# The last MLP's first matrix as seven block products of half-sized pieces, with sums of weights made by adding transfers

## The chip, the cores and the metric

The kernel runs on one core of a Trainium2 chip. The metric is the device time of one execution in microseconds (us). Before the change it is 2378.59 us, the median of 3 runs (2377.44 to 2379.38). The core's engines are TensorE (PE: matmuls; PEld is its weight load), VectorE (DVE), ScalarE (ACT), GpSimd (POOL) and SyncE (SP, which issues the DMAs here). Each runs its own queue in order.

## What is computed

A trunk of two layers over 1024 tokens of width 1024, in float32. Layer 0 mixes tokens with an mLSTM, layer 1 with latent attention over a shared K/V. Each mixer and each MLP stands between a norm with a modulation (scale and shift from a condition) and a norm with a gate. What the change touches is the MLP of the last layer (shortened):

```python
def sqrelu_mlp(h, w1, w2):                 # w1: 1024 x 4096, w2: 4096 x 1024
    return jnp.square(jax.nn.relu(h @ w1)) @ w2

for l in range(DEPTH):                     # two layers
    ...                                    # mixer
    h = modulate(rmsnorm(x, norm_g[l, 2]), sh2, sc2)
    y = sqrelu_mlp(h, mlp_w1[l], mlp_w2[l])
    x = x + g2[:, None, :] * rmsnorm(y, norm_g[l, 3])
return x
```

## The kernel before

**Precision.** Every large product is made of three fp32r matmuls: an operand is split into a rounded part `hi` and the rest `lo`, and `mm3` (L230) adds lo·hi, hi·lo and hi·hi into one PSUM tile (L231, L232, L233). Stationary tiles are 128x128, the moving operand is up to 512 columns wide.

**Weights.** `wload` brings 512 KB of weights (128x1024) into one of 4 `raw` buffers by a DMA on SP's queue; `wsplit` makes `wh` by a cast on ACT (L189) and `wl` by a subtraction on DVE (L190), in 8 buffers of the tag `ws`. The loads are issued AHEAD = 2 steps before their use.

**Stages.** Tokens are handled in two halves of 512 (`hfs[0]`, `hfs[1]`). Four MLP passes follow one another: `mlp(0, hfs[0])`, `mlp(0, hfs[1])`, `mlp(1, hfs[0])`, `mlp(1, hfs[1])`. `two_streams` runs the first three as a dense stream, between whose steps it puts the steps of mixers, of attention and of small preparations; the first has the preparation of latent weights beside it (`bg_latent`, which stores split weights to DRAM: the DMAs `lw<-wh` and `lw<-wl`). The last pass runs alone, with `all_out` (turning the residual stream into rows, `x_to_rows`, and the final norm, `rows_out`) between its steps.

**An MLP pass.** `mlp` makes a list of steps. A `hidden` step computes one of 32 blocks of 128 hidden features for 512 tokens: 8 blocks of input features, each `mm3` of 512 columns, so 24 matmuls into a PSUM tile `ps`; then relu (L962) and square (L963) on ACT, a cast (L471) on ACT and a subtraction (L472) on DVE give the two parts in `hd`. An `up` step multiplies hidden blocks with W2, 24 matmuls of 512 columns into `pm`, and adds the result to `y` (L198 on DVE). In the last pass the steps go in groups of four hidden blocks, and the `up` steps of a group stand between the hidden steps of the next one. A scheduler then orders each engine's instructions; `prompt` and `tc.high_priority` move weight loads and evacuations ahead, and `paced` holds others behind a given instruction. PSUM has two tiles each of `ps` and `pc` (one bank) and of `pm` (two banks).

Of the kernel before, what the change touches and what calls it, by code (L numbers as in the profile page):

```python
# [82 lines left out]
def kernel(  # L83
# [143 lines left out]

    pe_last = [None]

    def mm3(o, lh, ll, rh, rl, start, stop):  # L230
        nc.tensor.matmul(o, ll, rh, start=start, stop=False)  # L231
        nc.tensor.matmul(o, lh, rl, start=False, stop=False)  # L232
        pe_last[0] = nc.tensor.matmul(o, lh, rh, start=False, stop=stop)  # L233


    nc.scalar.preload_act_table_set("natural_log_exp_and_others")
# [240 lines left out]
    def normed(h, xs_, rstd, A, sh):  # L477

        for k in range(KD):
            with paced():  # L480
                nc.vector.scalar_tensor_tensor(
                    xs_[k], xs_[k], A[:, k : k + 1], rstd, ALU.mult, ALU.mult
                )
                split_mod(h.hi[k], h.lo[k], xs_[k], sh[:, k : k + 1])
            if k % 4 == 3:
                yield 1

# [455 lines left out]
    NF = DFF // P  # L943
    AHEAD = 2

    def mlp(l, hf, y, sizes, rows=False):


        w1, w2, h = mlp_w1[l], mlp_w2[l], hf.h2
        hids = {}  # L950

        def hidden(f):
            def hid(w):
                t = hdv(F32R)
                pt = ps()
                for k in range(KD):
                    if k == KD // 2:
                        yield "within"
                    mm3(pt, w[0][:, k], w[1][:, k], h.hi[k], h.lo[k], k == 0, k == KD - 1)
                s = tmp()  # L960
                with tc.high_priority(PRIO):
                    nc.scalar.activation(s, pt, AF.Relu)  # L962
                    nc.scalar.activation(s, s, AF.Square)  # L963
# [88 lines left out]
        steps, prev, f0 = [], [], 0  # L1052
        for G in sizes:
            fs = list(range(f0, f0 + G))
            f0, done = f0 + G, 0
            for i in range(G):
# [7 lines left out]
        for n in range(len(steps) + AHEAD):  # L1064
            if n < len(steps):
                ready.append(steps[n][0]())
            if n >= AHEAD:
                yield from steps[n - AHEAD][1](ready.pop(0))

                yield steps[(n - AHEAD + 1) % len(steps)][1].__name__  # L1070


    rope_d = scratch([2, P, S], "rope_d")
# [494 lines left out]

    def x_to_rows(half):

        for k in range(KD):
            a, b = tmc(), tmc()
            nc.sync.dma_start(a, xs_blk(k, half))
            yield
            pt = pc()
            for t in range(4):
                nc.tensor.transpose(pt[:, ts(t, P)], a[:, ts(t, P)], ident)
            nc.scalar.copy(b, pt)
# [19 lines left out]
    def rows_out(hf, y, B):  # L1598

        xt = []  # L1600
        for t in range(4):
            a = k4v()
            r0 = hf.i * H + t * P
            nc.sync.dma_start(a, xr[r0 : r0 + P, :].rearrange("p (a b) -> p a b", b=512))
            xt.append(a)
        yield
        for t in range(4):
            yt, st = y.t[t], small(4)
            for g in range(2):
                junk = ps()  # L1610
# [9 lines left out]
            for g in range(2):  # L1620
                nc.vector.scalar_tensor_tensor(ys[g], ys[g], r, xt[t][:, g], ALU.mult, ALU.add)
                r0 = hf.i * H + t * P
                nc.sync.dma_start(out[0, r0 : r0 + P, ts(g, 512)], ys[g])
            yield


# [126 lines left out]
    A1 = gain(2, NG(0, 2), adac(0, SC2))  # L1753
    B1 = gate(3, NG(0, 3), adac(0, G2))

    def post(hf, y, B, src, A, sh):
# [5 lines left out]
        yield 0  # L1762
        hf.h2 = Split()
        yield from normed(hf.h2, y, rstd, A, sh)

# [112 lines left out]
    def behind(fill, per):  # L1878

        more = True  # L1880
        while more:
            yield "align"
            more = some(fill, per)
            yield 1

    f0 = mlp(0, hfs[0], z0, [4] * 8)
    for n in range(20):
        if next(f0) != "within":
            next(p1, None)
    drain(p1)  # L1890
    two_streams(f0, behind(bg_latent(), 4))
    rope_perm()


    z1 = FH(claim=True)
    ya = [None, None]

    def mixer1(hf, z, attention):
# [12 lines left out]
        for _ in wout(b_w_out[0], hf.o, lambda m, pt: evac(y[m], pt)):  # L1911
            yield 0
        yield 1
        yield from post(hf, y, B2, x_cols, A3, adac(1, SH2))

    two_streams(mlp(0, hfs[1], z1, [2] * 14 + [4]), mixer1(hfs[0], z0, attention_first), bg_rest())


    u0 = FH(claim=True)
    two_streams(mlp(1, hfs[0], u0, [2] * 16, True), mixer1(hfs[1], z1, attention_second))  # L1920
    u1 = FH(claim=True)

    def all_out():
        yield from x_to_rows(0)
# [6 lines left out]

    fill = all_out()
    v = None
    dense = mlp(1, hfs[1], u1, [4] * 8, True)
    while (d := go(dense)) is not end:
        if v != "last" and d != "within":
            v = next(fill)
    drain(fill)

# [28 lines left out]
```

## Time and profile before

| what | us |
|---|---|
| median of 3 runs | 2378.59 |
| the profiled execution | 2377.5 |
| its span, first to last instruction | 2375.5 |
| POOL, L1346 memsets (32, attention's) | 6.6 |
| last pass, L472 on DVE (32) | 22.1 |
| last pass, L190 on DVE (61) | 74.6 |

The granted TensorE clock is 0.997 on average over the span. The profiled execution lies 1.1 us under the median of the runs. In a timeline a row gives start, duration, engine, line, operation and the tiles, output before input; what stands in square brackets is the time for which the engine had been idle and what ended that. Rows of matmuls overlap, since a matmul's duration runs to its end in the array; what one costs in a stream is read from start to start.

### The profile page before, as it was taken

To read this page: it belongs to the slowest core of one execution; us is meant where nothing else is said; L and a number is where in the kernel's file an instruction comes from. 1 tells how busy PE (TensorE), PEld (TensorE's weight loads), DVE (VectorE), ACT (ScalarE), POOL (GpSimd) and SP (SyncE) were. 2 spreads that over 40 slices of the span, in tenths; PEclk is the share of its full clock that TensorE was granted. 3 is DMA by queue.
4 is the path that set the end of the run, shared out by engine and by line. 5 is a ranking of instruction groups with operands and counts; after the bars stand their busy time and mean duration, and the time that the engine had idled before them with its cause. 6 is when DMAs were issued, how large, how long until landed. Compare 5 with 4: busy or idle time off the path is not lost.

```text
span 2375.5 us, 30534 instructions
## 1 busy us (share of the span) xinstructions
PE 2343.4 (99%) x11621; PEld 1946.7 (82%) x11621; DVE 1549.6 (65%) x2435; ACT 1055.6 (44%) x1716; POOL 18.2 (1%) x93
## 2 busy tenths in 40 slices
PE   7999999999999999999999999999999999999998
PEld 5888888788888888888888888888888888888887
DVE  6667866868666667877764967765666486353345
ACT  4355334655333454434443554444444453444333
POOL 1000000000000000000000000000000000000000
PEclk9999999999999999999999999999999999999999
DMA  9452664544664745555543454874434354364431
GB/s 313 149 142 85 186 181 139 168 133 144 186 181 143 250 135 187 160 161 183 182 133 113 147 166 163 249 248 136 148 98 143 114 169 129 102 191 140 144 102 62
DMA packets 377106, 374.48 MB, mean 158 GB/s; under 512 B 24355, under 2 KB 282464, under 8 KB 376960
## 3 DMA queue, kind: packets, MB, share of 16 engines
q1 hardware_dynamic: 376672, 372.44, 50.3%
q8 instruction: 91, 1.49, 0.3%
q14 instruction: 55, 0.45, 0.1%
q0 software_dynamic: 288, 0.10, 0.0%
HBM read 313.24 MB, written 59.24 MB: 157 GB/s over the span
## 4 chain that ended last, share of the span: by engine, by line
PE 89%; DVE 4%; DMA 4%; ACT 1%; issue 1%; SPq 0%; DVEq 0%; ACTq 0%
PE ps L231 16%; PE ps L233 16%; PE ps L232 16%; PE pm L231 9%; PE pm L232 9%; PE pm L233 9%; PE pc L1450 1%; DMA raw<-in_a_w_in_dram 1%; DMA raw<-in_mlp_w_dram 1%; PE pc L231 1%; PE pc L233 1%; PE pc L232 1%; PE pm L1336 1%; DVE wl L190 1%; PE pm L820 1%
## 5 line engine op out<-in xcount | busy, mean ns | idle before, releaser
L190 DVE TENSOR_TENSOR wl<-raw,wh 128x1024 fp32r<-128x1024 f32 (+2 forms) x366 | 438.9, 1202 | 442.7 <-ACT wh L189 435.7
L189 ACT CAST wh<-raw 128x1024 fp32r<-128x1024 f32 (+2 forms) x366 | 377.6, 1035 | 704.3 <-PE ps L231 381.7
L231 PE MATMUL ps<-k,wl 128*128 128x512 f32 x1528 | 605.2, 396 | 2.5 <-ACT k L679 1.4
L233 PE MATMUL ps<-k,wh 128*128 128x512 f32 x1528 | 596.1, 390 | 0.0
L232 PE MATMUL ps<-k,wh 128*128 128x512 f32 x1528 | 595.6, 390 | 0.0
L231 PEld LDWEIGHTS ps<-k,wl 128*128 128x128 f32 x1528 | 287.0, 188 | 65.1 <-issue 2.9
L233 PEld LDWEIGHTS ps<-k,wh 128*128 128x128 f32 x1528 | 286.8, 188 | 61.7 <-issue 0.5
L232 PEld LDWEIGHTS ps<-k,wh 128*128 128x128 f32 x1528 | 287.2, 188 | 58.8 <-issue 1.7
L198 DVE TENSOR_TENSOR k<-k,pm 128x512 f32<-128x512 f32 (+1 forms) x254 | 211.0, 860 | 104.1 <-PE pm L233 103.6
L231 PE MATMUL pm<-hd,wl 128*128 128x512 f32 x512 | 200.9, 392 | 0.5 <-ACT hd L471 0.5
L232 PE MATMUL pm<-hd,wh 128*128 128x512 f32 x512 | 199.3, 390 | 0.2 <-DVE hd L472 0.2
L233 PE MATMUL pm<-hd,wh 128*128 128x512 f32 x512 | 199.2, 389 | 0.0
L231 PE MATMUL pm<-wh,hd 128*128 128x512 f32 x488 | 192.2, 394 | 1.6 <-ACT raw L1342 1.3
L232 PE MATMUL pm<-wl,hd 128*128 128x512 f32 x488 | 190.9, 391 | 0.0
L233 PE MATMUL pm<-wh,hd 128*128 128x512 f32 x488 | 190.2, 390 | 0.0
L359 DVE SCALAR_TENSOR_TENSOR tma<-raw,cond,tma 128x512 f32<-128x512 f32 x168 | 125.6, 748 | 20.4 <-DMA raw<-in_kv_ada_w_dram 14.4
L472 DVE TENSOR_TENSOR hd<-tmp,hd 128x512 fp32r<-128x512 f32 x128 | 88.3, 690 | 54.7 <-ACT hd L471 54.4
L1342 ACT ACTIVATE raw<-pm,sm 128x128 f32<-128x128 f32 (+3 forms) x64 | 47.5, 742 | 150.1 <-DVE sm L1341 121.8
L231 PEld LDWEIGHTS pm<-hd,wl 128*128 128x128 f32 x512 | 96.2, 188 | 20.8 <-ACT hd L471 0.9
L232 PEld LDWEIGHTS pm<-hd,wh 128*128 128x128 f32 x512 | 96.1, 188 | 20.5 <-DVE hd L472 0.5
L233 PEld LDWEIGHTS pm<-hd,wh 128*128 128x128 f32 x512 | 96.1, 188 | 20.2
L231 PEld LDWEIGHTS pm<-wh,hd 128*128 128x128 f32 x488 | 91.6, 188 | 22.3 <-ACT raw L1342 3.5
(354 smaller groups left out, 3426.2 us busy)
## 6 DMA issues: line engine op xcount, KB each, us to landing
raw<-in_mlp_w_dram SPq DMA_DIRECT2D x256, 512.0 KB, 4.2
raw<-in_ada_w_dram SPq DMA_DIRECT2D x80, 512.0 KB, 4.2
raw<-in_a_w_in_dram SPq DMA_DIRECT2D x48, 512.0 KB, 4.8
xs<-k SPq DMA_DIRECT2D x40, 256.0 KB, 4.8
raw<-in_kv_ada_w_dram SPq DMA_DIRECT2D x16, 512.0 KB, 4.0
raw<-in_a_w_out_dram SPq DMA_DIRECT2D x16, 512.0 KB, 4.8
kd<-k SPq DMA_DIRECT2D x32, 256.0 KB, 3.8
vd<-k SPq DMA_DIRECT2D x32, 256.0 KB, 4.5
```

What stands on the lines that cost most here:

```text
L189: nc.scalar.copy(hi[:, :n], r[:, :n])
L190: i = nc.vector.tensor_sub(lo[:, :n], r[:, :n], hi[:, :n].bitcast(F32))
L198: return f(*a, **k)
L231: nc.tensor.matmul(o, ll, rh, start=start, stop=False)
L232: nc.tensor.matmul(o, lh, rl, start=False, stop=False)
L233: pe_last[0] = nc.tensor.matmul(o, lh, rh, start=False, stop=stop)
L359: nc.vector.scalar_tensor_tensor(acc, r[:, kk], cond[:, k : k + 1], acc, ALU.mult, ALU.add)
L472: nc.vector.tensor_sub(lo, u, hi.bitcast(F32))
L820: nc.tensor.matmul(nv[:, r, i], hf.PT[p_][:, r, cs], v[2 * p_ + r], start=g == 0, stop=True,)
L1336: nc.tensor.matmul(o[:, :w], qh, kh, start=False, stop=True)
L1342: nc.scalar.activation(pr[:, :n], f, AF.Exp, bias=m, scale=SCALE, accum_out=l)
L1450: nc.tensor.transpose(pt[:, ts(2 * e + i, P)], u.prs[i][:, ts(b + e, P)], ident)
```

## The change

It replaces the first product of the last pass, `h @ w1` for the second half of the tokens, by seven products of half-sized blocks, in the manner of Strassen and Winograd. The input is cut into four pieces: input features in two halves of 512 (kh) and tokens in two quarters of 256 (th). W1 is cut into four as well: its 1024 rows in two halves and its 4096 columns in two halves (f). Seven products of sums of such pieces give all four blocks of the result, where the plain way takes eight.

- `quarters` makes the pieces and sums of the input. It stands in place of the plain split behind the norm of `hfs[1]`, during `mlp(1, hfs[0])`; its `rest` (pieces 7, 5 and 4) is issued at dense step 61 of that pass. Each piece is split into its two parts.
- `weight_sums` makes the four sums of weight blocks in DRAM (`sums`), by 32 DMAs of 1 MB on GpSimd's queue, 128 rows of 8 KB each or one contiguous copy; 16 of them add to what is in their target. Ahead of each stands a one-element memset on DVE, which is paced, and a copy on POOL that reads it. `with_weight_sums` issues one every third dense step of both `mlp(0, ...)` passes.
- `pair(p_)` computes hidden blocks p_ and 16 + p_ in four steps: `first` (products 1, 2), `second` (6, 7), `third` (5, 4) and `fourth` (3). A product is 4 blocks of features, each `mm3` of 256 columns: 12 matmuls. `fourth` is moved behind `first` of the next pair. The sums between products are made in PSUM by accumulation, and by additions on DVE with copies by ACT.
- `up_by_f` is the `up` step of two hidden blocks each, kept in four PSUM banks over two steps.
- Smaller edits: in this pass loads are issued three steps ahead, and `all_out` goes on at every second dense step; `x_to_rows` fetches one block ahead; `rows_out` writes its unused squares to a `tmc` tile (before: `ps`) and fetches its rows later; `u1` has no memset to claim it.

```diff
+    def weight_sums(w):
...
+            ops = [
+                (1, part(1, 0, c), 0), (2, part(1, 0, c), 0),
+                (1, part(0, 0, c), 1), (2, part(1, 1, c), 1),
+                (0, o(1), 0), (0, part(1, 1, c), 1), (3, o(0), 0), (3, part(0, 1, c), 1),
+            ]
+            for i, src, add in ops:
+                flag, seen = small(1), small(1)
+                with paced():
+                    nc.vector.memset(flag, 0.0)
+                now = nc.gpsimd.tensor_copy(seen, flag)
+                with tc.issue_after(now.ins):
+                    if add:
+                        nc.gpsimd.dma_start(o(i), src, accum_op=ALU.add)
+                    else:
+                        nc.gpsimd.dma_start(o(i), src)
+                yield
...
+            def product(i, o, w, start=False):
+                (wh, wl), (bh, bl) = w, B[i]
+                for k in range(4):
+                    mm3(o, wh[:, k], wl[:, k], bh[k], bl[k], start and k == 0, k == 3, more=not start)
...
+            def first(w):
+                u.b, u.x, u.s, u.r = cut(ps()), cut(pc()), tmp(), tmp()
+                product(1, u.b, w[0], True)
+                with tc.high_priority(PRIO):
+                    u.s1 = cut(tmc())
+                    nc.scalar.copy(u.s1, u.b)
+                product(2, u.x, w[1], True)
+                with tc.high_priority(PRIO):
+                    c = cut(u.s)
+                    nc.vector.tensor_add(c, u.s1, u.x)
+                    nc.scalar.activation(c, c, AF.Relu)
...
+            def finish(f, s):
+                t = hdv(F32R)
+                nc.scalar.activation(s, s, AF.Square)
+                split_mod(t[:, 0], t[:, 1], s, None)
+                hids[f] = (t[:, 0], t[:, 1])
...
+            def third(w):
+                product(5, u.b, w[0])
+                with tc.high_priority(PRIO):
+                    nc.vector.tensor_add(u.r[:, N:], u.s7, u.b)
+                product(4, u.z, w[1])
+                with tc.high_priority(PRIO):
+                    nc.vector.tensor_add(cut(u.r), u.s16, u.z)
+                    nc.scalar.activation(u.r, u.r, AF.Relu, scale=-1.0)
+                    finish(f1, u.r)
...
+            def fourth(w):
+                product(3, u.b, w)
+                with tc.high_priority(PRIO):
+                    nc.scalar.activation(u.s[:, N:], u.b, AF.Relu)
+                    finish(p_, u.s)
...
+            for i in range(0, G if B else 0, 2):
+                p1, p2, p3, p4 = pair(a + i // 2)
+                ups = [up_by_f(prev, i + e, False) for e in range(2) if prev]
+                final = a + i // 2 == NF // 2 - 1
+                steps += [p1] + late + ups[:1] + [p2]
+                steps += [p3, p4] + ups[1:] if final else ups[1:] + [p3]
+                late = [p4]
...
+    two_streams(with_weight_sums(mlp(0, hfs[1], z1, [2] * 14 + [4])), mixer1(hfs[0], z0, attention_first), bg_rest())
```

PE's order, in the last pass, where four transposes of `x_to_rows` stand between two steps. `k` are the parts of the input, `wh` and `wl` of the weights. Before, an `up` step (into `pm`) is followed by a hidden step (into `ps`) of 24 matmuls 128x512:

```order
L231 MATMUL pm_17764<-wh_17600,hd_17440 128x512
L232 MATMUL pm_17764<-wl_17601,hd_17440 128x512
L233 MATMUL pm_17764<-wh_17600,hd_17440 128x512
L1577 MATMUL pc_17791<-ident,tmc_17749 128x128 x4
L231 MATMUL ps_17805<-k_2964_16827,wl_17715 128x512
L232 MATMUL ps_17805<-k_2965_16828,wh_17714 128x512
```

Now, at such a place, product 4 of a pair (into `pc`, with `wh` and `wl` of `third`) ends, and product 1 of the next pair (into `ps`) follows; `mm3` is at L232 to L234:

```order
L232 MATMUL pc_18522<-k_3090_17380,wl_18487 128x256
L233 MATMUL pc_18522<-k_3091_17381,wh_18486 128x256
L234 MATMUL pc_18522<-k_3090_17380,wh_18486 128x256
L1763 MATMUL pc_18622<-ident,tmc_18479 128x128 x4
L232 MATMUL ps_18636<-k_3039_17080,wl_18519 128x256
L233 MATMUL ps_18636<-k_3040_17081,wh_18518 128x256
L234 MATMUL ps_18636<-k_3039_17080,wh_18518 128x256
```

A hidden step of 24 wide matmuls has become products of 12 half-wide ones; behind this place stand product 2 (into `pc`), product 3 of the pair before (into the `ps` of that pair), and an `up` step.

DVE's order at the end of a group in the last pass. Before, a hidden step costs it one instruction (L472, the `lo` part), between weight splits (L190) and the additions to `y` (L198):

```order
L472 TENSOR_TENSOR hd_18765<-tmp_18791,hd_18765 128x512
L190 TENSOR_TENSOR wl_18808<-raw_18805,wh_18807 128x1024
L198 TENSOR_TENSOR k_3033_17286<-k_3033_17286,pm_18811 128x512
L198 TENSOR_TENSOR k_3034_17287<-k_3034_17287,pm_18811 128x512
L190 TENSOR_TENSOR wl_18848<-raw_18845,wh_18847 128x1024
```

Now the additions behind products 5 (L1056), 4 (L1059) and 2 (L1029) stand among the splits, and the `lo` part (L473) of the block that product 4 ends:

```order
L1056 TENSOR_TENSOR tmp_18421<-tmc_18549,ps_18418 128x256
L190 TENSOR_TENSOR wl_18633<-raw_18629,wh_18632 128x1024
L1059 TENSOR_TENSOR tmp_18421<-tmc_18535,pc_18522 128x256
L1779 TENSOR_SCALAR tmc_18692<-ident,mods 128x128 x4
L1779 TENSOR_SCALAR tmc_18700<-ident,mods 128x128 x4
L190 TENSOR_TENSOR wl_18671<-raw_18668,wh_18670 128x1024
L1029 TENSOR_TENSOR tmp_18638<-tmc_18652,pc_18637 128x256
L473 TENSOR_TENSOR hd_18617<-tmp_18421,hd_18617 128x512
```

The addition L1059, which frees the PSUM tile of product 4, has a split of weights directly ahead of it, and `lo` has another split and the next pair's addition L1029 ahead.

POOL's order during `mlp(0, hfs[1])`. Before, only attention's memsets stand there (then L1346). Now the copies (L985) and the transfers of `weight_sums` (L990 plain, L988 adding) stand between them (L1528):

```order
L985 COPY sm_8233<-sm_8232 128x1
L990 DMA sums_134<-sums_135 16x16384
L1528 MEMSET raw_8495 128x128
L985 COPY sm_8486<-sm_8485 128x1
L988 DMA sums_134<-in_mlp_w_dram 128x2048
L1528 MEMSET raw_8524 128x128
L1528 MEMSET raw_8662 128x128
L1528 MEMSET raw_8691 128x128
L985 COPY sm_8757<-sm_8756 128x1
L990 DMA sums_137<-sums_134 16x16384
```

A memset of attention now stands behind a transfer of the sums that is issued before it.

More of the change, by code (lines that the diff above doesn't have):

```diff
@@ L944, with part @@
     AHEAD = 2
-    def mlp(l, hf, y, sizes, rows=False):
-        w1, w2, h = mlp_w1[l], mlp_w2[l], hf.h2
-        hids = {}
+    FH_ = DFF // 2
+    by_k = lambda t: t.rearrange("p (a b) -> p a b", b=P)
+    sums = [scratch([H, FH_], f"sums{i}") for i in range(4)]
+    def weight_sums(w):
+        def part(f, kh, c):
+            r0 = kh * H + c * P
+            return w[r0 : r0 + P, f * FH_ : (f + 1) * FH_]
+        for c in range(4):
+            o = lambda i: sums[i][ts(c, P)]
+            ops = [
[5 more added lines that the diff above has]
+                flag, seen = small(1), small(1)
+                with paced():
+                    nc.vector.memset(flag, 0.0)
[6 more added lines that the diff above has]
+                yield
@@ L1051, in mlp @@
         up = up_rows if rows else up_cols
-        steps, prev, f0 = [], [], 0
+        steps, late, prev, f0 = [], [], [], 0
         for G in sizes:
@@ L1063, in mlp @@
         ready = []
-        for n in range(len(steps) + AHEAD):
+        early = AHEAD + bool(B)
+        for n in range(len(steps) + early):
             if n < len(steps):
                 ready.append(steps[n][0]())
-            if n >= AHEAD:
-                yield from steps[n - AHEAD][1](ready.pop(0))
-                yield steps[(n - AHEAD + 1) % len(steps)][1].__name__
+            if n >= early:
+                yield from steps[n - early][1](ready.pop(0))
+                yield steps[(n - early + 1) % len(steps)][1].__name__
     rope_d = scratch([2, P, S], "rope_d")
@@ L1762, in post @@
         yield 0
+        if kept:
+            yield from kept(y, rstd)
+            return
         hf.h2 = Split()
@@ L1884, in behind, with with_weight_sums @@
             yield 1
+    wsums = weight_sums(mlp_w1[1])
+    def with_weight_sums(g):
+        n = 0
+        for v in g:
+            n += v != "within"
+            if v != "within" and n % 3 == 2:
+                next(wsums, None)
+            yield v
     f0 = mlp(0, hfs[0], z0, [4] * 8)
@@ L1890, with quarters, part, rest @@
     drain(p1)
-    two_streams(f0, behind(bg_latent(), 4))
+    two_streams(with_weight_sums(f0), behind(bg_latent(), 4))
     rope_perm()
+    B = {}
+    later = [None]
+    def quarters(y, rstd):
+        q = lambda kh, th, j: y.t[2 * kh + j][:, :, ts(th, 256)]
+        sub = nc.vector.tensor_sub
+        def part(i, kh, th):
+            t = [k4v(F32R, 256), k4v(F32R, 256)]
+            for j in range(2):
+                s = ts(j, 2)
+                split_wide(t[0][:, s], t[1][:, s], q(kh, th, j))
+            B[i] = [[a[:, k] for k in range(4)] for a in t]
+        yield from normed_kept(y, rstd, A3, adac(1, SH2))
+        part(1, 0, 0)
+        part(2, 1, 0)
+        yield 1
+        minus = lambda o, a: nc.vector.scalar_tensor_tensor(
+            o, a, -1.0, o, ALU.mult, ALU.subtract
+        )
+        for j in range(2):
+            sub(q(0, 0, j), q(0, 0, j), q(0, 1, j))
+        part(3, 1, 1)
+        for j in range(2):
+            sub(q(0, 1, j), q(1, 1, j), q(0, 1, j))
+            minus(q(1, 1, j), q(0, 0, j))
+        part(6, 1, 1)
+        for j in range(2):
+            minus(q(1, 0, j), q(1, 1, j))
+        def rest():
+            part(7, 0, 1)
+            part(5, 0, 0)
+            part(4, 1, 0)
+        later[0] = rest
+        yield 1
     z1 = FH(claim=True)
@@ L1933 @@
     v = None
-    dense = mlp(1, hfs[1], u1, [4] * 8, True)
+    dense = mlp(1, hfs[1], u1, [4] * 8, True, B)
+    n = 0
     while (d := go(dense)) is not end:
-        if v != "last" and d != "within":
+        n += d != "within"
+        if v != "last" and d != "within" and n % 2:
             v = next(fill)
```

137 lines of the change are left out of this document (120 added, 17 removed).

## The prediction

> **What bounds the kernel now.** I read the page first: busy time, the slices, the chain that ended last.
>
> ```profile
> span 2375.5 us, 30534 instructions
> PE 2343.4 (99%) x11621; PEld 1946.7 (82%) x11621; DVE 1549.6 (65%) x2435; ACT 1055.6 (44%) x1716; POOL 18.2 (1%) x93
> PE 89%; DVE 4%; DMA 4%; ACT 1%; issue 1%; SPq 0%; DVEq 0%; ACTq 0%
> q1 hardware_dynamic: 376672, 372.44, 50.3%
> raw<-in_mlp_w_dram SPq DMA_DIRECT2D x256, 512.0 KB, 4.2
> ```
>
> TensorE (PE) is busy 99% of the span and makes 89% of the chain. What shortens its stream shortens the kernel, unless a wait appears; what the other engines gain or lose counts only where PE then waits. The hardware DMA queue holds 50.3% of the 16 engines, and a weight tile lands 4.2 us after its issue. Then the same by stage (start:end of the window, its length, busy time of PE, PEld, DVE, ACT, POOL, clock, DMA share, GB/s):
>
> ```profile
> 433.00:862.00 429.00, 426.67 (x1888) 350.88 (x1887) 290.01 (x392) 196.41 (x267) 0.94 (x8) 1.00 0.55 167
> 862.00:1400.00 538.00, 535.64 (x2580) 445.15 (x2579) 395.06 (x600) 246.45 (x404) 4.03 (x24) 1.00 0.51 159
> 1955.00:2010.00 55.00, 55.00 (x252) 45.42 (x251) 37.29 (x51) 21.57 (x30) 0.39 (x4) 1.00 0.48 140
> 2100.00:2200.00 100.00, 100.00 (x449) 82.03 (x448) 53.54 (x90) 44.47 (x77) 0.00 (x0) 1.00 0.55 169
> 2200.00:2300.00 100.00, 100.00 (x449) 82.76 (x448) 37.94 (x45) 35.30 (x47) 0.00 (x0) 1.00 0.40 126
> ```
>
> The first two windows are layer 0's MLP, where the sums of weights are put; the last two lie in the last MLP, about 2010 to 2367 us. There PE has no gap at all, at a granted clock of 1.00, while DVE is busy 38 to 54 us in 100 and ACT 35 to 44.
>
> **The products: fewer columns, at a worse price per column.** A step `hid` is 8 feature blocks of 3 matmuls 128x512, so 32 steps are 768 of them. The change puts 16 pairs × 7 products × 4 blocks × 3 = 1344 matmuls 128x256 in their place: 344,064 columns for 393,216, an eighth less. Busy means do not give the price, because matmuls overlap; the starts do. The timeline of PE (start, duration) where it streams the one form and the other, and a window, in the columns of those above, of small matmuls with stalls:
>
> ```profile
> 149.72 0.39 PE L233 MATMUL ps<-k,wh 128*128 128x512 f32 x1
> 149.95 0.39 PE L231 MATMUL ps<-k,wl 128*128 128x512 f32 x1
> 150.18 0.39 PE L232 MATMUL ps<-k,wh 128*128 128x512 f32 x1
> 150.40 0.39 PE L233 MATMUL ps<-k,wh 128*128 128x512 f32 x1
> ...
> 88.68 0.28 PE L231 MATMUL ps<-wh,k 128*128 128x256 f32 x1
> ...
> 91.56 0.28 PE L231 MATMUL ps<-wh,k 128*128 128x256 f32 x1
> ...
> 100.00:120.00 20.00, 19.46 (x156) 17.30 (x155) 14.00 (x25) 7.97 (x23) 0.00 (x0) 1.00 0.37 107
> ```
>
> From 149.72 to 150.40 are three steps of 0.227 us. From 88.68 to 91.56 are 24 matmuls of the half width, three to a block: 0.120 us each. That is 53% of the full one, not half. So 768 × 0.227 = 174.3 us become 1344 × 0.120 = 161.3 us: **−13.0 us**. The bounds: −21.8 if cost followed the columns (an eighth of 174.3), and −2 if a half-width one cost the 20.00 / 156 = 0.128 us of the last row (1344 × 0.128 = 172), where other forms and 0.5 us of idle time are among them. I take the measured pitch. The second matrix keeps its 512-wide matmuls and their number.
>
> The Trainium skill, "TensorE: Matmul & The Clock Gate", section "Back-to-back issue gap", lists 262 cycles for 256 columns and 518 for 512. By that ratio of 0.506 the new stream would cost 1344 × 0.506 × 0.227 = 154.4 us, an estimate, and the saving would be 19.9. The starts above show 0.53, so this trace speaks against it.
>
> **More weight tiles.** W1 takes 3.5 tiles of 1024 columns a pair (the last is half a tile) where two `hid` steps took 2, so 24 more splits in the last MLP, each a cast on ACT and a subtraction on DVE:
>
> ```profile
> L189 ACT CAST wh<-raw 128x1024 fp32r<-128x1024 f32 x350 | 366.9, 1052 | 694.5 <-PE ps L231 381.3 <-DMA raw<-in_mlp_w_dram 103.6 <-PE pm L231 73.7
> L190 DVE TENSOR_TENSOR wl<-raw,wh 128x1024 fp32r<-128x1024 f32 x350 | 426.9, 1222 | 438.1 <-ACT wh L189 433.5 <-PE ps L233 2.7 <-DMA lw<-wl 1.0
> L669 DVE COPY k<-ps 128x256 f32<-128x256 f32 x12 | 5.0, 421 | 4.4 <-PE ps L233 4.4
> L671 ACT COPY k<-ps 128x256 f32<-128x256 f32 x12 | 4.5, 374 | 28.7 <-PE ps L233 28.7
> ```
>
> 24 × 1.05 = 25 us on ACT and 24 × 1.22 = 29 us on DVE, over some 350 us. A pair also brings three half-wide copies on ACT (1.1 us) and three half-wide additions on DVE (about 1.3 us by the 421 ns row), 18 and 20 us in all. DVE goes from 0.38–0.54 to about 0.52–0.68, ACT from 0.35–0.44 to about 0.47–0.56. In sum that fits beside PE: cost nothing. It would cost if it came in a lump, which is the next part.
>
> **New waits in the last MLP.** Before, PE waited for `hd` only through this chain (timeline of the last MLP, behind a step that ended about 2263.6):
>
> ```profile
> 2264.13 0.59 ACT L962 ACTIVATE tmp<-ps 128x512 f32<-128x512 f32 x1
> 2264.76 0.63 ACT L963 ACTIVATE tmp<-tmp 128x512 f32<-128x512 f32 x1
> 2265.42 0.62 ACT L471 CAST hd<-tmp 128x512 fp32r<-128x512 f32 x1
> 2266.07 0.69 DVE L472 TENSOR_TENSOR hd<-tmp,hd 128x512 fp32r<-128x512 f32 x1 [0.58 <-ACT hd L471]
> ```
>
> It was 3.2 us long, and a whole step (5.4 us) stood between it and its reader. Now the hidden block of the upper half is ready only after product P4: half-wide addition on DVE (0.42 and some 0.3 of handoff), relu and square on ACT (0.63 each), cast (0.62), `lo` on DVE (0.69), about 3.6 us with the handoffs. In DVE's new order a weight split of 1.22 us stands ahead of the addition, and a second, with the addition of the next pair's P2, ahead of `lo`: 3.6 to 6.0 us. The reader at a group's start is the second block of the next `up`. Between are four transposes (0.4), P1, P2 and P3 (12 × 0.120 = 1.44 each) and three 512-wide matmuls (0.68): 5.4 us. So PE waits between 0 and 0.6 us at each of the 7 group changes. The other handoff: P2 of the next pair needs the PSUM tile that P4's addition reads. That is free 1.65 us after P4 when a split stands ahead (1.22 + 0.42), and P2 starts 1.85 us after it with the transposes between, 1.44 without. It costs 0 to 0.2, 15 times. Sum of bounds: 0 to 7.2 us, and 16 × 1.22 = 19.5 us if a whole split came late in every pair. I take **+3.5**, the middle of the narrower pair, since every handoff has most of its time covered. `first` has an addition of P2 queued on DVE; splits of weights stand behind it there, and they run some 10 us ahead of use.
>
> **The tail.** The last chain of before:
>
> ```profile
> 2366.99 0.69 DVE L198 TENSOR_TENSOR k<-k,pc 128x512 f32<-128x512 f32 x1 [0.30 <-PE pc L233]
> 2368.92 0.68 DVE L1616 TENSOR_TENSOR tmc<-k,k 128x512 f32<-128x512 f32 x1
> 2369.77 0.15 DVE L1618 TENSOR_SCALAR sm<-sm 128x1 f32<-128x1 f32 x1
> 2371.01 1.41 DVE L1621 SCALAR_TENSOR_TENSOR tmc<-tmc,sm,k 128x512 f32<-128x512 f32 x2
> ```
>
> L1618 ends 2.2 us after the last accumulation (2367.68). In the new order both gain products of the last rows (0.69 each), three small operations (0.15 each) and the scaling of the rows before (1.41) stand between them: 3.4 us. **+1.0**, within 0 and 1.2.
>
> **The sums of weights.** 32 transfers of 1 MB on GpSimd's queue, 16 of them adding, one every third dense step of both MLPs of layer 0. At 372.44 MB for 50.3% of the span, a plain copy is about 1 × 0.503 × 2375.5 / 372.44 = 3.2 us of all 16 engines; an adding one reads its target too, and I bound it by double, 6.4. Together 51 + 102 = 153 us of 967: the share there goes from 0.53 to about 0.69. No average is in danger. What counts is a weight tile with no time to spare. Before, the stretch that prepares the latent weights is the tightest:
>
> ```profile
> 745.00:802.00 57.00, 57.00 (x254) 46.60 (x253) 48.23 (x78) 24.61 (x32) 0.00 (x0) 1.00 0.76 231
> PEld ps L231 <- DVE wl L190: 0.8, 5, 0.2
> lw<-wl SPq DMA_DIRECT2D x5, 512.0 KB, 5.6
> ```
>
> The five waits of PE's weight load for `wl` come with DVE busy 48 us of 57: splits end just as they are read, and they reuse buffers that the store `lw` reads. A step is 5.5 us, so three or four transfers fall here, and each can push one split by 0 to 6.4 us: 0 to 22 us. Elsewhere the splits run 3 to 14 us ahead of their first matmul by their starts, more than one transfer mostly takes. I take **+2.0**, a third of one such delay, near the low end because PE has five waits of 0.2 us there and none for a DMA. The 32 tiny DVE and POOL operations cost nothing: POOL was busy 4 us of 538. An adding transfer makes POOL wait for the one before it, and attention's memsets are queued behind; that one was issued three steps earlier, 16 us at least, so it has landed.
>
> The Trainium skill, "DMA: Bandwidth & Descriptors", section "Queues, rings and completion order", says that an engine takes turns between its queue rows, a packet at a time. By that a weight tile beside a sum would land in about twice its 4.2 us, an estimate, and the stretch above would cost up to 4 × 4.2 = 17 us; no row of before shows two loaded queues.
>
> **Quarters of the input.** Their 14 half-tile splits (about 0.62 us on ACT, 0.69 on DVE) and the sums stand beside the MLP before, where DVE has 37.29 busy of 55 and PE no gap: nothing, or about 5 us if the first quarter came late; it is finished steps ahead.
>
> **Sum** against the profiled execution of 2377.5 us (2375.5 of span and 2.0 around it): −13.0 + 3.5 + 1.0 + 2.0 = −6.5, so 2371.0. The median of the runs shown is 2378.6, 1.1 above that execution: **2372 us**.
>
> **The rivals.**
> *Nothing is given back*: every handoff is covered. For it: PE had no gap in the last MLP; against: 5.4 against up to 6.0 us. Time 2378.6 − 13.0 = 2365.6.
> *Cost by columns*: the stream saves 20 to 22 us, 2360 with the waits. Against it the 0.120 us; the skill's table is this rival.
> *The pair's chain takes it back*: products of 1.44 us are too short to cover a 1.22 us split and a handoff, and PE loses some 0.8 us a pair: 16 × 0.8 = 12.8 for −13.0; about 2378. For it: DVE works in order with splits ahead of the additions; against: two products and often an `up` step (5.4) stand between most writers and readers.
> *Slower, by the sums*: the adding transfers delay weight loads and stores wherever splits are just in time. The point is a delay past the lead: with 3 us lost at 6 of the 32 transfers, or 22 us in the tight stretch, the balance turns: +18 to +22 for −8.5 before, 2388 to 2392. For it: share 0.76 and 5.6 us stores there; against: most tiles have 4 to 14 us of lead.
> *The products don't do what they say* (order or number different): the built order has the 1344.
>
> **How the numbers follow.** About 0.2%, 4.8 us, is what a measurement tells from no change. Forecast (−4 to −10): 0.47, of which a tenth or so is under 4.8. Nothing given back: 0.14. By columns: 0.03. Chain takes it back (−3 to +4): 0.17. Slower by the sums (+5 to +22): 0.19. So faster 0.42 + 0.14 + 0.03 = 0.59, same 0.05 + 0.16 = 0.21, slower 0.20. The range goes from the full saving, 2364, to half of the slower case, 2388; beyond lie the columns' rival and the other half.
>
> **What would show it.** The pitch of the 128x256 matmuls in the last MLP (0.120), and that stage shorter by 8 to 10 us from its first matmul to the last; PE's idle time before `pc` and `pm` there, released by DVE, a few us; the time at which the last MLP begins: later by about 2 us if the sums are cheap, by over 10 if they collide, then with waits of PE's weight load for `wl` near 750 to 800 us and landings far above 4.2 us. The prediction is wrong if the pitch is not 0.120, if PE waits over 0.5 us a pair, or if the last MLP begins over 8 us late.

## The result and the profile after

| | us |
|---|---|
| before, median | 2378.6 (2377.4 to 2379.4, 4 runs) |
| changed, median | 2393.7 (2389.4 to 2395.9, 4 runs) |
| ratio | 1.0062 (95% interval 1.0044 to 1.0079) |
| profiled execution of the change, and its span | 2395.9, 2394.1 |

The change makes the kernel slower by about 15 us, where the prediction said faster by 6.5. The profiled execution of the change is the slowest of its four runs and that of the kernel before the fastest of its own, so the two spans differ by 18.6 us where the medians differ by 15.1. The page after, its lines on busy time, the chain, the software queue and the transfers of the sums:

```profile
span 2394.1 us, 32205 instructions
PE 2339.1 (98%) x12197; PEld 1966.8 (82%) x12197; DVE 1602.3 (67%) x2561; ACT 1098.6 (46%) x1826; POOL 50.4 (2%) x153
PE 82%; DMA 7%; DVE 7%; ACT 2%; issue 1%; SPq 0%; DVEq 0%; ACTq 0%
q0 software_dynamic: 4000, 33.66, 5.6%
sums<-in_mlp_w_dram POOLq DMA_DIRECT2D x24, 1024.0 KB, 8.8
```

PE's busy time fell by 4.3 us and the span grew by 18.6. So the stream did get shorter, and new idle time outweighs it: the chain of work that ended last has 7% of DMA and 7% of DVE, where it had 4% each.

Since TensorE's order up to the last pass is nearly the same (some steps of attention beside the second `mlp(0, ...)` have moved), the lag is read by finding the same matmul in both timelines. First the reduction of a modulation vector (L339 before, L340 after), then a score product of attention (L1330, L1512), then the last matmul of all. Before:

```profile
667.90 0.33 PE L339 MATMUL pc<-ident,tma 128*128 128x128 f32 x1
...
1205.02 0.42 PE L1330 MATMUL pm<-k,k 128*128 128x384 f32 x1
...
2366.57 0.39 PE L233 MATMUL pc<-wh,hd 128*128 128x512 f32 x1
```

After:

```profile
678.21 0.47 PE L340 MATMUL pc<-ident,tma 128*128 128x128 f32 x1 [8.27 <-DVE tma L360]
...
1225.58 0.34 PE L1512 MATMUL pm<-k,k 128*128 128x384 f32 x1
...
2384.55 0.39 PE L234 MATMUL pc<-wh,hd 128*128 128x512 f32 x1
```

The lag is 10.3 us at the first, 20.6 at the second, 18.0 at the last. By two matmuls behind attention (1942.71 before, 1967.79 after) it had grown to 25.1, so the last pass won 7.1 us back. What TensorE waited for between 640 and 1240 us (in total, times, longest) was, before:

```profile
PE pm L1330 <- DVE k L198: 1.7, 3, 0.7
PE pc L339 <- DVE tma L359: 1.0, 1, 1.0
```

and after:

```profile
PE pc L340 <- DVE tma L360: 8.3, 1, 8.3
PE pm L1512 <- DVE k L198: 5.1, 4, 3.0
PE ps L232 <- DVE wl L190: 2.7, 2, 2.2
PE ps L233 <- DVE hd L473: 1.4, 2, 1.1
PE pm L1512 <- DVE sm L984: 0.6, 1, 0.6
```

2.7 us became 18.1. All are waits for DVE, though DVE is busy only 67% of the span. The longest one, in the timeline of the other engines and queues (a row that ends in x2 or x3 spans several instructions):

```profile
658.09 0.81 POOL L988 DMA_DIRECT2D sums<-in_mlp_w_dram  x1
...
663.50 3.81 SPq L211 DMA_DIRECT2D raw<-in_mlp_w_dram  x2
...
672.26 1.04 ACT L189 CAST wh<-raw 128x1024 fp32r<-128x1024 f32 x1 [8.23 <-DMA raw<-in_mlp_w_dram]
673.34 1.23 DVE L190 TENSOR_TENSOR wl<-raw,wh 128x1024 fp32r<-128x1024 f32 x1 [7.02 <-ACT wh L189]
...
674.48 1.21 DVE L198 TENSOR_TENSOR k<-k,pm 128x1024 f32<-128x1024 f32 x1
...
675.61 0.75 DVE L360 SCALAR_TENSOR_TENSOR tma<-raw,cond,tma 128x512 f32<-128x512 f32 x1
...
677.41 0.74 DVE L360 SCALAR_TENSOR_TENSOR tma<-raw,cond,tma 128x512 f32<-128x512 f32 x1
```

An adding transfer is issued at 658.1. A weight tile issued at 663.5 can be cast only at 672.3, 8.8 us later. At this place before, the same tile took 4.3 us:

```profile
657.64 1.82 SPq L211 DMA_DIRECT2D raw<-in_mlp_w_dram  x2
...
661.94 1.05 ACT L189 CAST wh<-raw 128x1024 fp32r<-128x1024 f32 x1 [3.76 <-DMA raw<-in_mlp_w_dram]
```

That slow landing is 4.5 us of the tile's delay; it was also issued 5.9 us later than before, when TensorE was only 1.9 us behind. A load of weights starts when a split has freed one of the four `raw` buffers (the split ahead ends at 663.48, the load is issued at 663.50), so lateness is handed on from tile to tile. Most of it began at the adding transfer of 620.0 us: the weight tile issued at 623.3 beside it was cast 9.7 us later, where its like before (620.50 to 625.59) took 5.1.

The split of the tile of 663.5 is not needed yet. But DVE runs in order, and behind the split stand the steps of the modulation (L360), which TensorE's next instruction reads. So a late tile with time to spare stops TensorE through what is queued behind its split.

The Trainium skill, "DMA: Bandwidth & Descriptors", section "Queues, rings and completion order", has each DMA engine take turns between the queue rows that have work for it. By that, as an estimate, a tile beside a loaded queue takes about twice as long; 4.3 became 8.8 us for this tile and 5.1 became 9.7 for the earlier one, and the trace agrees.

### The profile page after: what moved, and what is told of

It reads as the page before. It is cut to its first block, busy times and chain, and to the rows that moved or that the text cites. A ratio compares the mean times of both kernels' runs of the same rounds, so it can differ in the third digit from the quotient of the medians.

```text
span 2394.1 us, 32205 instructions
## 1 busy us (share of the span) xinstructions
PE 2339.1 (98%) x12197; PEld 1966.8 (82%) x12197; DVE 1602.3 (67%) x2561; ACT 1098.6 (46%) x1826; POOL 50.4 (2%) x153
## 4 chain that ended last, share of the span: by engine, by line
PE 82%; DMA 7%; DVE 7%; ACT 2%; issue 1%; SPq 0%; DVEq 0%; ACTq 0%
PE ps L232 14%; PE ps L233 14%; PE ps L234 14%; PE pm L232 9%; PE pm L233 8%; PE pm L234 8%; DMA raw<-in_mlp_w_dram 5%; PE pc L232 2%; PE pc L233 2%; PE pc L234 2%; DVE wl L190 2%; PE pc L1632 1%; ACT wh L189 1%; DMA raw<-in_a_w_in_dram 1%; DVE tma L360 1%
## 5 line engine op out<-in xcount | busy, mean ns | idle before, releaser
L190 DVE TENSOR_TENSOR wl<-raw,wh 128x1024 fp32r<-128x1024 f32 (+2 forms) x382 | 458.5, 1203 | 410.8 <-ACT wh L189 354.6
L189 ACT CAST wh<-raw 128x1024 fp32r<-128x1024 f32 (+2 forms) x382 | 394.0, 1035 | 682.5 <-PE ps L232 232.9
L232 PE MATMUL ps<-k,wl 128*128 128x512 f32 (+1 forms) x1464 | 560.1, 383 | 5.6 <-DVE wl L190 4.0
L234 PE MATMUL ps<-k,wh 128*128 128x512 f32 (+1 forms) x1464 | 551.5, 377 | 0.0
L233 PE MATMUL ps<-k,wh 128*128 128x512 f32 (+1 forms) x1464 | 551.3, 377 | 0.0
L232 PEld LDWEIGHTS ps<-k,wl 128*128 128x128 f32 x1464 | 276.2, 189 | 61.0 <-DVE wl L190 6.4
L234 PEld LDWEIGHTS ps<-k,wh 128*128 128x128 f32 x1464 | 276.1, 189 | 51.7 <-issue 0.5
L233 PEld LDWEIGHTS ps<-k,wh 128*128 128x128 f32 x1464 | 276.5, 189 | 50.2 <-issue 1.7
L198 DVE TENSOR_TENSOR k<-k,pm 128x512 f32<-128x512 f32 (+1 forms) x254 | 210.9, 859 | 85.9 <-PE pm L234 85.4
L232 PE MATMUL pm<-hd,wl 128*128 128x512 f32 x512 | 201.0, 393 | 0.6 <-ACT hd L472 0.5
L232 PE MATMUL pm<-wh,hd 128*128 128x512 f32 x488 | 194.0, 398 | 6.3 <-DVE hd L473 4.1
L234 PE MATMUL pm<-hd,wh 128*128 128x512 f32 x512 | 199.2, 389 | 0.0
L234 PE MATMUL pm<-wh,hd 128*128 128x512 f32 x488 | 190.3, 390 | 0.0
L360 DVE SCALAR_TENSOR_TENSOR tma<-raw,cond,tma 128x512 f32<-128x512 f32 x168 | 125.6, 748 | 24.2 <-DMA raw<-in_kv_ada_w_dram 13.6
L232 PEld LDWEIGHTS pm<-wh,hd 128*128 128x128 f32 x488 | 91.7, 188 | 28.9 <-DVE hd L473 6.5
L473 DVE TENSOR_TENSOR hd<-tmp,hd 128x512 fp32r<-128x512 f32 x128 | 87.9, 688 | 39.5 <-ACT hd L472 39.1
L232 PEld LDWEIGHTS pm<-hd,wl 128*128 128x128 f32 x512 | 96.2, 188 | 21.3 <-ACT hd L472 0.9
L234 PEld LDWEIGHTS pm<-hd,wh 128*128 128x128 f32 x512 | 96.1, 188 | 20.1
```

What stands on the lines that cost most here:

```text
L189: nc.scalar.copy(hi[:, :n], r[:, :n])
L190: i = nc.vector.tensor_sub(lo[:, :n], r[:, :n], hi[:, :n].bitcast(F32))
L198: return f(*a, **k)
L232: nc.tensor.matmul(o, ll, rh, start=start, stop=False, **m)
L233: nc.tensor.matmul(o, lh, rl, start=False, stop=False, **m)
L360: nc.vector.scalar_tensor_tensor(acc, r[:, kk], cond[:, k : k + 1], acc, ALU.mult, ALU.add)
```

## The experiments

Each time is beside runs of the kernel before on the same chip: 2377.95 us for the first four experiments, 2378.36 for the two runs that split the memsets and copies by pass, 2378.27 for the early places and the run beside it, and 2378.24 for the other four. What is quoted is the median of the runs; a trace is one of them, and can lie some us off it.

### Without the transfers

The memsets and copies stay; the products read blocks of W1 in place of the sums.

```diff
-                with tc.issue_after(now.ins):
-                    if add:
-                        nc.gpsimd.dma_start(o(i), src, accum_op=ALU.add)
-                    else:
-                        nc.gpsimd.dma_start(o(i), src)
...
-                    wload([(4 * e, 0, wcols(sums[i + e], p_ * P, P, 0, 4)) for e in range(2)], P)
+                    wload([(4 * e, 0, wcols(w1, p_ * P, P, 4 * e, 4)) for e in range(2)], P)
```

> The changed kernel with its 32 transfers of the sums left out (the one-element memsets and copies stay) and the products reading W1's own blocks in place of the sums, so the output is another one. Theory A, the transfers delay weight loads and splits in layer 0's MLPs: 2369 to 2374 us, the last pass still about 7 us shorter than before, and no PE idle time over 1.5 us between 600 and 1250 us. Rival B, the loss comes from the extra memsets and copies on DVE and POOL and from the order that they change: within 3 us of the changed kernel, 2391 to 2396. Rival C, the last pass is what loses: also near 2393.

2377.5 us (ratio 0.9996, 0.9987 to 1.0004). Theory A takes 16 us of the loss; B and C do not hold for these 16. But 2369 to 2374 was missed too: without any transfer the change gained nothing. Its trace still lagged 3.8 us behind before at the score product of 1205 us, so something beside the transfers costs there.

### The sums alone

The kernel before, with the 32 transfers at the same steps of both passes, and nothing else of the change.

```diff
-    two_streams(f0, behind(bg_latent(), 4))
+    two_streams(with_weight_sums(f0), behind(bg_latent(), 4))
...
-    two_streams(mlp(0, hfs[1], z1, [2] * 14 + [4]), mixer1(hfs[0], z0, attention_first), bg_rest())
+    two_streams(with_weight_sums(mlp(0, hfs[1], z1, [2] * 14 + [4])), mixer1(hfs[0], z0, attention_first), bg_rest())
```

> The kernel before with the 32 transfers (and their memsets and copies) alone; nothing reads the sums. Theory A: before plus 18 to 25 us, 2397 to 2404. Rivals B and C differ: B gives the same as A here, C gives before within 3 us, 2379 to 2382.

2397.6 us (1.0082, 1.0067 to 1.0096): before plus 19.6, as A had it. The last pass is not the cause, and the whole loss is there without it.

### All transfers plain

```diff
-                        nc.gpsimd.dma_start(o(i), src, accum_op=ALU.add)
+                        nc.gpsimd.dma_start(o(i), src)
```

> The changed kernel with the 16 adding transfers as plain copies, in the same order on every engine (the sums are wrong, so the output is another one). If the adding is what costs (9.8 us to landing for 7.1 of a plain one): 6 to 14 us less than the changed kernel, 2380 to 2388. If 1 MB in one piece is what costs, adding or not: within 3 us of it.

2380.5 us (1.0011, 1.0002 to 1.0019): 13.2 less than the changed kernel, at the upper end of what was expected, with the same order on every engine. The 16 instructions that had added, L988, took 9.8 us to landing in the changed kernel and 6.1 here (medians). The adding costs nearly all that the transfers cost. Plain transfers aren't free at these places, though: the trace (2384.7 us, 4.1 over the median) still has a wait of 4.4 us at the modulations.

### The sums one pass later

The transfers go into `mlp(1, hfs[0])`, three at every five dense steps.

```diff
-    two_streams(with_weight_sums(f0), behind(bg_latent(), 4))
+    two_streams(f0, behind(bg_latent(), 4))
...
                 n += 1
+                if n * 3 % 5 < 3:
+                    next(wsums, None)
```

> The changed kernel with the 32 transfers moved into mlp(1, hfs[0]), the pass after, at three of every five dense steps; all is computed. That pass has neither the preparation of latent weights nor of the modulations beside it. Theory A with the cost tied to the place: 2372 to 2382. If a transfer costs its 0.6 us of delay wherever it stands: 2390 or more.

2380.9 us (1.0013, 1.0004 to 1.0021), within the expected 2372 to 2382, near its upper end. TensorE ran level with before up to 1560 us and lost some 10 us from there to 1860, in this pass's attention. The place matters, and this is not the right one.

### The last pass alone

No transfers, no memsets, no copies; the products read blocks of W1. TensorE's order is that of before up to the last pass.

```diff
-    two_streams(with_weight_sums(f0), behind(bg_latent(), 4))
+    two_streams(f0, behind(bg_latent(), 4))
```

> The changed kernel with no work for the sums at all (no transfers, memsets or copies; the products read W1's own blocks, so the output is another one). TensorE's order is that of before up to the last pass. If the extra memsets and copies, through the order that they change, cost the 4 us that the run without transfers still lost between 950 and 1210 us: 2371 to 2374. If that loss has to do with the last pass's edits: 2376 to 2379.

2372.0 us (0.9973, 0.9962 to 0.9985): 6.2 us faster than before, and 5.5 less than with the memsets and copies left in. So these cost, and the last pass gains.

### The memsets and copies alone

The kernel before with the 32 one-element memsets on DVE and copies on POOL, without transfers.

```diff
                 now = nc.gpsimd.tensor_copy(seen, flag)
-                with tc.issue_after(now.ins):
-                    if add:
-                        nc.gpsimd.dma_start(o(i), src, accum_op=ALU.add)
-                    else:
-                        nc.gpsimd.dma_start(o(i), src)
                 yield
```

> The kernel before with the 32 memsets on DVE and copies on POOL alone, no transfers. If they cost 4 us through the order: 2381 to 2384. If they are free: 2377 to 2380.

2385.1 us (1.0025, 1.0015 to 1.0035): before plus 6.8, more than expected. On DVE a memset is busy for 0.06 us. What TensorE waits for between 640 and 1240 us in this run:

```profile
PE pc L339 <- DVE tma L359: 3.4, 2, 2.2
PE pm L1356 <- DVE k L198: 2.0, 3, 0.9
PE ps L232 <- DVE hd L472: 1.0, 1, 1.0
PE pm L1356 <- DVE sm L968: 0.6, 1, 0.6
```

7.0 us in these rows in place of 2.7. The scheduler, given 32 more instructions that are held to a place, ordered others around them differently, on DVE from the first of them on and on TensorE from 890 us on, in attention. Whether the order is what costs has to be told place by place. Two later runs split this by the pass they stand in: in the first kernel `with_weight_sums` is left only around `f0`, in the second only around the other `mlp(0, ...)`.

> The kernel before with the memsets and copies alone, and only the 17 in the first mlp(0, ...). TensorE's order is that of before; DVE's differs around 640 to 680 us. The run with all of them lost 2.5 us there: 2379.5 to 2382 if that is DVE's order, 2377.5 to 2379 if it was chance.

2380.1 us (1.0007, 0.9998 to 1.0017): +1.8, not told from nothing. The time lies in the range that was named for "DVE's order", but the trace speaks against that. PE, DVE and ACT run the same instructions in the same order here as with all 32 memsets and copies up to 850 us; this trace lost 0.3 us there, where that one lost 3.5 at the modulations. So the order doesn't explain that part, the largest wait in the rows above; its cause is open.

> The kernel before with the memsets and copies alone, and only in the second mlp(0, ...), 21 of them. TensorE's order of attention's steps differs from before as in the run with all of them, which lost about 4 us between 950 and 1210 us: 2381 to 2384 if the order costs, 2377.5 to 2379 if it does not.

2383.3 us (1.0018, 1.0009 to 1.0027): +5.0. The second pass's share is the larger, and it is the one in which TensorE's order of attention's steps had changed. Three traces with this order (this run, all 32, and the change without transfers) lost 3.2 to 3.9 us between 880 and 1240 us. That the two medians sum to the 6.8 is in part chance, since the trace of all 32 lost half of it at the modulations. Whether it is TensorE's order or DVE's in that pass that costs was not separated.

### Chosen places

10 transfers at steps 22, 25, ... of the first `mlp(0, ...)`, 6 late in the second, 16 in `mlp(1, hfs[0])`, of which 13 at consecutive steps beside attention.

```diff
-    def with_weight_sums(g):
+    def with_weight_sums(g, at):
...
-            if v != "within" and n % 3 == 2:
+            if v != "within" and n in at:
```

> The changed kernel with the 32 transfers at places where the trace of the changed kernel and that of the later placing show no stall: 10 in the first mlp(0, ...) behind the modulations, 6 at the end of the second, 16 in mlp(1, hfs[0]) away from the start of its attention. If the loss is a matter of splits just in time: 2371 to 2376. If every transfer costs its 0.6 us: 2388 or more.

2381.2 us (1.0009, 1.0000 to 1.0017): missed. The trace is level with before until 1680 us and then loses 8 us by 1750, among the 13. DVE's timeline there:

```profile
1678.19 1.23 DVE L190 TENSOR_TENSOR wl<-raw,wh 128x1024 fp32r<-128x1024 f32 x1 [4.02 <-ACT wh L189]
1679.34 0.82 DVE L1522 TENSOR_REDUCE sm<-pm 128x1 f32<-128x640 f32 x1
1680.19 0.15 DVE L1523 TENSOR_SCALAR sm<-sm 128x1 f32<-128x1 f32 x1
```

DVE waits 4.0 us for a weight tile, and the softmax (L1522 and on) stands behind: the same mechanism at another place. By 1686 us half of the 8 us is lost. In the changed kernel this pass had no sums, and its window was

```profile
1640.00:1840.00 200.00, 198.67 (x1124) 170.26 (x1125) 122.37 (x206) 84.27 (x148) 2.67 (x13) 1.00 0.37 126
```

A DMA share of 0.37 did not make the stretch safe.

### The order of the last pass

On top of the chosen places, in `mlp`:

```diff
-                steps += [p1] + late + ups[:1] + [p2]
+                steps += [p1] + late + [p2] + ups[:1]
```

> The kernel of those chosen places, and in the last pass the steps second (products 6 and 7) and the first up step of a pair change places, so that the hidden block of product 4 has 2.9 us more before its reader. The trace of the changed kernel has 3 waits of 1.3 to 1.5 us for it. If they go: 3 to 4.5 us less than with the chosen places alone. If the wait only moves to another tile: within 1.5 us of it.

2374.2 us (0.9988, 0.9978 to 0.9998): 7.0 less than the chosen places alone, more than the 3 to 4.5 expected. This row of the changed kernel's waits, which the trace with the chosen places has too (4.1 us, 3 times), is gone from it:

```profile
PE pm L232 <- DVE hd L473: 4.1, 3, 1.5
```

No other wait took its place in the last pass. In the two traces the last pass is 6.0 us shorter with the new order, of 6.2 in all (a lead of 1.6 us at 1610 us was gone by 1760). So the idle time of these waits is not all that they cost.

### Early places

15 transfers at every second step of the first `mlp(0, ...)` behind the modulations, 9 at the end of the second, 8 at the start of `mlp(1, hfs[0])`, none beside attention; with the new order of steps.

```diff
+    two_streams(with_weight_sums(f0, range(22, 51, 2)), behind(bg_latent(), 4))
...
+    two_streams(with_weight_sums(mlp(0, hfs[1], z1, [2] * 14 + [4]), range(46, 64, 2)), mixer1(hfs[0], z0, attention_first), bg_rest())
...
+            with_rest(mlp(1, hfs[0], u0, [2] * 16, True)), [2, 3, 5, 7, 8, 10, 11, 12]
```

> All is computed. The 32 transfers stand at 15 steps of the first mlp(0, ...) behind the modulations, 9 at the end of the second, and 8 at the start of mlp(1, hfs[0]), none in the attention that cost the chosen places 8 us; the last pass has the changed order of steps. TensorE's order up to the last pass is that of before. If place and order are what the sums cost: 2366 to 2371, faster than before by 0.3 to 0.5%. If transfers cost wherever they stand: 2376 or more.

> The last pass alone, without any work for the sums (the products read W1's own blocks, so the output is another one), and with the changed order of its steps. It is the floor for what the sums may cost: 2372.0 less the 4.1 us of the three waits, 2366 to 2369. The early places should lie 0 to 3 us above it if the sums are hidden there.

The early places: **2366.9 us** (0.9953, 0.9939 to 0.9966), faster than before by 11 us and than the change by 27. The last pass with the new order and no sums at all: 2367.9 (0.9961, 0.9948 to 0.9973). By the medians the sums cost nothing that these runs can tell. By the traces that is in part chance: with the early places TensorE lost 2.3 us at 802 us, with a wait of 2.1 us for a weight split soon after a transfer, and the trace without sums lost 3.8 us at 1576 us, at a wait for `k<-td` that is only 0.5 us with the early places. Windows of the early places' trace, over the three stretches that hold all but the first three transfers and over the last pass:

```profile
700.00:862.00 162.00, 159.88 (x707) 131.63 (x706) 97.40 (x142) 62.18 (x82) 11.50 (x24) 1.00 0.89 258
1240.00:1400.00 160.00, 159.32 (x698) 130.65 (x697) 99.90 (x127) 72.55 (x102) 11.46 (x24) 1.00 0.68 197
1400.00:1560.00 160.00, 159.96 (x743) 132.44 (x742) 118.24 (x179) 80.04 (x128) 6.78 (x15) 1.00 0.81 251
1985.00:2355.00 370.00, 369.98 (x2292) 333.72 (x2292) 218.26 (x324) 192.26 (x338) 0.00 (x0) 1.00 0.54 165
```

With a DMA share of 0.89 TensorE idles 2.1 us in 162, and in the last pass not at all. The transfers land no sooner (11.2 us, median, for the adding ones). The reading that fits is that little stands behind the splits here that TensorE needs at once; no run isolates it, so it is not shown.

## Why the prediction was wrong

**The products** (−13.0): right. The starts in the last pass after:

```profile
2034.20 0.28 PE L234 MATMUL ps<-k,wh 128*128 128x256 f32 x1
...
2036.00 0.28 PE L234 MATMUL pc<-k,wh 128*128 128x256 f32 x1
```

15 matmuls in 1.80 us, 0.120 each. The rival by columns, and with it the ratio of 0.506, is out.

**New waits in the last pass** (+3.5): the place was right, the size somewhat small. They are the 4.1 us above, at 3 of the 7 group changes, and at the place named: the second hidden block of a group, whose `lo` part came late. The row at the first of them is

```profile
2060.30 0.50 PE L232 MATMUL pm<-wh,hd 128*128 128x512 f32 x1 [1.28 <-DVE hd L473]
```

It was put at 0 to 0.6 us each and is 1.3 to 1.5: on ACT a weight cast of 1.04 us (at 2056.95) stood ahead of the block's own cast, which the working left out. And the price is more than the idle time: from the start of the matmul ahead (2058.63) to that of this one are 1.67 us, where 0.23 is usual. Without these waits the last pass is 6.0 us shorter in the traces, and the kernel by 4.1 us (from the last pass alone) or 7.0 us (from the chosen places) by medians.

**The tail** (+1.0): right, though the parts of its 3.4 us add up to 3.2; from the start of the last matmul to the end of the span it is 9.55 us after and 8.93 before, 0.6 more, and 1.1 more in the last pass alone.

**More splits, quarters of the input** (0): no wait in the traces is theirs, but they were not run apart. For the last pass alone −13.0 + 3.5 + 1.0 = −8.5 was forecast, and −6.2 measured. In its trace the last pass itself won 6.0 us, less than forecast because of the dearer waits. Ahead of it 3.2 us were lost near 1576 us, in attention, where TensorE waited 2.0 us for a load (`k<-td`) that had cost 0.5 before, and then ran at half its pitch for some 3 us. This wait is longer than before in other runs with and without transfers too, and was not settled.

**The sums of weights** (+2.0): this term failed, and it is most of the miss: 19.6 us when done alone. Two steps of its working failed.

The first is "The 32 tiny DVE and POOL operations cost nothing". Alone they cost 6.8 us. Their busy time is nothing; but the order that a scheduler makes around them was not looked at as a price. 5.0 us of it come with those in the second pass, where steps of attention moved; the rest is not told from nothing.

The second is that the place was looked for where splits are just in time for TensorE, the stretch of the latent weights, and the +2.0 is a third of one delay there. There, the window after has no gap at all, at a DMA share of 0.75:

```profile
640.00:681.00 41.00, 32.14 (x139) 25.88 (x138) 23.74 (x32) 13.15 (x18) 2.80 (x6) 0.92 0.76 231
681.00:940.00 259.00, 259.00 (x1141) 212.74 (x1140) 171.59 (x247) 110.69 (x153) 13.36 (x26) 1.00 0.75 228
```

The loss stood just before it, in the modulations, and later in attention. The lead that counts is not that of the split before its own matmul, 3 to 14 us, but that of whatever is queued behind the split on DVE. By the prediction's own sign, a last MLP that begins over 8 us late, this shows at once: it began 25.1 us late. The rival "slower, by the sums" had the direction, the size (18 to 22 us of loss) and what is delayed (weight loads) right, its place wrong; and it had been given 0.19.

The transfers themselves cost 2397.6 − 2385.1 = 12.5 us. The parts add up to −6.2 + 6.8 + 12.5 = +13.1, with +15.1 measured.

**POOL behind an adding transfer** (0): right for TensorE. It did wait, 3.6 us at 813 us, for the transfer issued at 802.1, with nothing of attention behind it. So the 16 us between transfers that the working counted on are not kept everywhere.

## What to carry to other kernels

When a background transfer makes loads late, ask for each load not when its own result is needed, but what stands behind the first instruction that waits for it, on an engine that runs in order. A DMA share says little about this: 0.89 cost one wait of 2.1 us at one place, and at another, where the share without the sums was 0.37, the transfers cost 8 us. Instructions that are put in only to mark a time can cost more than their busy time (5.0 us here, with the order that a scheduler made around them), so compare the order first, and move them to where it stays the same.

## What the hardware showed

**A stall can be paid twice.** After the idle 2.2 us at 947 to 949 us TensorE first ran at its usual pitch, and 1.5 us later at half of it, for 3 us:

```profile
950.02 0.40 PE L232 MATMUL ps<-k,wl 128*128 128x512 f32 x1
950.25 0.39 PE L233 MATMUL ps<-k,wh 128*128 128x512 f32 x1
...
951.63 0.63 PE L234 MATMUL ps<-k,wh 128*128 128x512 f32 x1
952.06 0.63 PE L232 MATMUL ps<-k,wl 128*128 128x512 f32 x1
```

The pitch is 0.23 us in the first pair and 0.43 in the second. The lag grew by 2.5 us with the stall and by 1.5 more at that pitch; the granted clock is 0.72 from 949 to 955 us. The granted clock of 0.92 in the window 640 to 681 us, above, is the same after the stall of 8.3 us. Not every stall does this: behind the wait of 3.0 us at 1061 us in the same trace, and behind one of 2.8 us at 1749 us with the chosen places, the granted clock stays at 1.00. What decides it was not tested.

**An adding DMA is slower to land than a plain one**: 9.8 us for 6.1, for the same 1 MB at the same places and in the same order, and the kernel was 13.2 us slower with it, at these places. At the early places it lands no sooner (11.2 us) and the medians show no cost.
